# Front of a hybrid encoder layer: values of heads 0-3 ahead of the last convolution chunk, scores that don't wait for values, the squares of the queries by one operation

## The chip, the cores and the metric

The kernel runs on one core of one Trainium2 chip. The metric is the device time of one execution in microseconds (us), lower is better. The kernel before was run three times: 1312.26 us in the median, 1311.49 to 1314.74.

## What is computed

One encoder layer over 256 rows of 2048 numbers, all in float32 (cut to what matters here):

```python
u = rms_norm(h) @ w_in                      # 2048 -> 5120
u_conv, u_attn = split(u)                   # 2 x 1024 | queries, keys, values: 3 x 1024
# group A: a * sigmoid(b), 31 taps along the rows, layer norm, silu
# group B: 8 heads, each with two sets of queries and keys of 64, values of 128
q, k = rms_norm(q) / 8, rms_norm(k)         # over each 64
p = softmax(where(mask, q @ k.T, -inf))     # two maps a head
o = rms_norm((p[0] - lam * p[1]) @ v)       # over each 128
h = h + concat([conv, o]) @ w_out           # 2048 -> 2048
y = h + moe(rms_norm(h))                    # 32 experts, the top 2 of one of 4 groups
```

## The kernel before

The kernel has a front (norm, input projection, convolution, attention, output projection, router) and a back, in which 16 pairs of experts pass one after another: every pair streams its gate, up and down weights through a ring of nine tiles of 2 MB, and its matmuls follow the loads. The ring's tiles are buffers of the front, reused: a load starts when the front has let go of its buffer (lines 979 to 1010).

**Steps.** The front's two projections are 112 steps. Steps 0 to 79 are the input projection: ten groups of 512 columns, eight steps each, in the order that ORDER (line 26) gives. A group is a convolution chunk ("c", 256 of the 1024 channels with their gates), or queries, keys or values of four heads ("q", "k", "v"; 0 is heads 0-3, 1 is heads 4-7). Steps 80 to 111 are the output projection: part 0 (heads 0-3, steps 80 to 87), part 1 (heads 4-7, 88 to 95) and part "c" (the convolution, 96 to 111), each over four groups of 512 columns. Weights come in tiles of 2 MB, one for four steps. A step has 12 matmuls of 512 columns (lines 714 to 716): float32 is split into a rounded half and its rest, and three products of the four are taken. The split of a step's weights (`split`, lines 665 and 666) is a copy on ScalarE and a subtraction on VectorE; it is issued two steps ahead, one step ahead in the output projection, into one of three buffers.

**The planner.** All engines but SP run in the order in which the code issues instructions, and everything besides steps is issued by a small planner while the kernel is built. Work is a set of generators ("units"), each of which yields the engine it needs next (A ScalarE, D VectorE, P TensorE) with a cost in us, and waits by W (a number of steps) or C (a condition of the plan; no engine waits there). In each step `vector_phase` adds PACE_A to ScalarE's room and PACE_V to VectorE's, and what TensorE's own units took before, and issues units in order of priority while there is room; unused room is not kept. VectorE's room that no unit needs goes to taps of the convolution (`fill`, TAP us each; 31 taps for each of 8 blocks of 128 channels, line 325, the first of a block line 322), from one list in the order of the chunks. After a step's matmuls `tensor_phase` issues P units that are ready. A unit that changes its engine goes on one step later at the earliest, except P of a "quick" one.

**Units of the change.** `queries` (lines 433 to 452): for each of two tiles of 128 rows a scaled copy out of PSUM (441), then `squares` (line 430): for each of eight pieces of 64 columns one Square on ScalarE that also sums; the inverse roots for the scale of the scores by bit tricks and three Newton steps on GpSimd (146 to 150, 169 to 171); four transposes (420) and copies (451). `keys` (454 to 478): squares, inverse roots, scaled by VectorE (466), transposed. `values` (480 to 485): a scaled copy. `attend` (one for tile 0, two for tile 1, for each set of four heads): scores by matmul (499), mask and negative maximum on VectorE (506 to 508), exponential with its sum on ScalarE (517), the difference of the two maps on VectorE (525 to 534), transposes (540), a copy (544), the product with the values (554). `attend_norm`: squares of the result (430 again), inverse root on GpSimd, scale (570, 572), transposes (420), rounded half (579) and rest (581) for the output projection. `conv_norm` takes the mean over channels when the last taps are done (362, 366), subtracts it (370), squares, variance (381), inverse root (390), and `conv_out` finishes in four pieces (403 to 410). `finish` adds the projection to the input rows (611), transposes the sum (617) for the router (626).

**What waits.** Before each part of the output projection the plan waits (`idle_until`) until both norms of that part's heads, or a piece of the convolution, have been issued: rounds without a step, each with two warming matmuls (line 245) and room of 2.5 us for ScalarE and VectorE.

Of the kernel before, what the change touches and what calls it, by code (L numbers as in the profile page):

```python
# [14 lines left out]
AF = mybir.ActivationFunctionType  # L15
ALU = mybir.AluOpType
AX = mybir.AxisListType

EPS = 1e-6
S, D = 256, 2048  # L20
NT = 2
# [1 line left out]
DC = 1024  # L23
TAPS = 31

ORDER = [('c', 0), ('c', 1), ('c', 2), ('k', 0), ('k', 1), ('q', 0), ('c', 3), ('v', 0), ('q', 1), ('v', 1)]
NH, HD, VD = 8, 64, 128
NE, NG, EPG = 32, 4, 8
DE = 512
# [1 line left out]
C = 64  # L31
LAM_INIT = 0.8 - 0.6 * math.exp(-0.3 * 0)
NEG = -1.0e30
PACE_A, PACE_V = 1.3, 1.25
PARTS = (0, 1, "c")
TAP = 0.38
IDLE = 2.5
SC_AT = 4
PIECES = ((0, 256), (256, 384), (384, 512))
# [18 lines left out]
def block_kernel(ctx, tc, x, xT, par, w_in, w_out, w_gu, w_dn, out):  # L58
# [81 lines left out]
    def tmp(shape=(128, 512)):  # L140
        i = free_tmps.pop(0)
        return i, wk.tile(list(shape), F32, name=f"t{i}", bufs=1)
# [281 lines left out]
    def squares(ps, ssq, scale):  # L424

        i, sq = tmp()
        w = 512 // ssq.shape[1]
        for j in range(ssq.shape[1]):
            c = slice(j * w, (j + 1) * w)
            nc.scalar.activation(sq[:, c], ps[:, c], AF.Square, scale=scale(j), accum_out=ssq[:, j:j + 1])  # L430
        free_tmps.append(i)

    def queries(half, ps):

        ssq = sm.tile([128, NT * 8], F32, name="qs")
        hs = slice(4 * half, 4 * half + 4)
        ys = []
        for t in range(NT):
            yield "A", 2.9, 2
            i, y = tmp()  # L440
            nc.scalar.activation(y, ps[t][1], AF.Copy, scale=rstd1[:, t:t + 1])
            squares(ps[t][1], ssq[:, 8 * t:8 * t + 8], lambda j: rstd1[:, t:t + 1])
            free_banks.append(ps[t][0])
            if t == 1:
                rstd_bits(ssq, HD, rq[:, half].rearrange("p t h r -> p (t h r)"), "k", nc.gpsimd)
            yield "P", 1, 0.44
            b0, tv = turn(y, i)
            yield "A", 1.1, 0
            for r in range(2):
                p = slice(64 * r, 64 * r + 64)  # L450
                nc.scalar.activation(qz[r][p, hs, t * 128:(t + 1) * 128], tv[p], AF.Copy, scale=qg[p, 0:1])
            free_banks.append(b0)

    def keys(half, ps):
        ssq = sm.tile([128, NT * 8], F32, name="qs")
        hs = slice(4 * half, 4 * half + 4)
        for t in range(NT):
            yield "A", 2.3, 1
            squares(ps[t][1], ssq[:, 8 * t:8 * t + 8], lambda j: rstd1[:, t:t + 1])
        rk = rstd_bits(ssq, HD, sm.tile([128, NT * 8], F32, name="rk"), "k", nc.gpsimd)  # L460
        yield "W", 2
        ys = []
        for t in range(NT):
            yield "D", 0.65, 1
            ys.append(tmp())
            nc.vector.scalar_tensor_tensor(ys[t][1].rearrange("p (h d) -> p h d", d=HD),
                                           ps[t][1].rearrange("p (h d) -> p h d", d=HD), rstd1[:, t:t + 1],
                                           rk[:, 8 * t:8 * t + 8, None].to_broadcast([128, 8, HD]),
                                           op0=ALU.mult, op1=ALU.mult)
            free_banks.append(ps[t][0])  # L470
        tvs = []
        for t in range(NT):
            yield "P", 1, 0.44
            tvs.append(turn(ys[t][1], ys[t][0]))
        for t in range(NT):
            yield "A", 0.6, 0
            nc.scalar.activation(kT[:, hs, t * 128:(t + 1) * 128], tvs[t][1], AF.Copy, scale=P("kg"))
            free_banks.append(tvs[t][0])
# [8 lines left out]
    def attend(t, g, s, st):  # L487

        nk = t + 1
        K = nk * 128  # L490
        nh = 4 // nk
        h0 = 4 * g + s * nh
        yield "P", 2, 0.9
        pv = []
        for r in range(2):
            b0, ps = bank()
            v = ps.rearrange("p (h k) -> p h k", k=K)
            for j in range(nh):
                nc.tensor.matmul(v[:, j], qz[r][:, h0 + j, t * 128:(t + 1) * 128], kT[:, h0 + j, 0:K],  # L499
                                 start=True, stop=True)  # L500
            pv.append((b0, v))
        nm = sm.tile([128, 2, 2, 4], F32, name="nm", bufs=4)
        for r in range(2):
            yield "D", 1.0, 0
            b0, v = pv[r]
            nc.vector.memset(v[0:64, :, K - 64:K], NEG)
            nc.vector.tensor_reduce(nm[:, r, 0, :nh], v, axis=AX.X, op=ALU.max, negate=True)
            nc.vector.tensor_tensor(nm[:, r, 1, :nh], nm[:, r, 0, :nh], rq[:, g, t, s * nh:s * nh + nh, r],
                                    op=ALU.mult)
        pe = []  # L510
        for r in range(2):
            yield "A", 0.25 * nh + 0.6, 2 - r
            b0, v = pv[r]
            i, p = tmp()
            pp = p.rearrange("p (h k) -> p h k", k=K)
            for j in range(nh):
                nc.scalar.activation(pp[:, j], v[:, j], AF.Exp, bias=nm[:, r, 1, j:j + 1],
                                     scale=rq[:, g, t, s * nh + j, r:r + 1],
                                     accum_out=esum[:, t, r, h0 + j:h0 + j + 1])
            free_banks.append(b0)  # L520
            pe.append((i, pp))
        yield "D", 1.4, 0
        (i0, p0), (i1, p1) = pe
        c = sm.tile([128, 2, 4], F32, name="c", bufs=4)
        nc.vector.reciprocal(c[:, 0, :nh], esum[:, t, 1, h0:h0 + nh])
        nc.vector.scalar_tensor_tensor(c[:, 1, :nh], c[:, 0, :nh], nlam, esum[:, t, 0, h0:h0 + nh],
                                       op0=ALU.mult, op1=ALU.mult)
        for j in range(nh):
            nc.vector.scalar_tensor_tensor(p0[:, j], p1[:, j], c[:, 1, j:j + 1], p0[:, j],
                                           op0=ALU.mult, op1=ALU.add)  # L530
        free_tmps.append(i1)
        if s == t:
            st["rs0"] = sm.tile([128, 4], F32, name="rs0", bufs=4)
            nc.vector.reciprocal(st["rs0"], esum[:, t, 0, 4 * g:4 * g + 4])
        yield "P", 1, 0.44
        b0, tp = bank()
        tv = tp.rearrange("p (h k q) -> p h k q", k=nk, q=128)
        for j in range(nh):
            for kt in range(nk):
                nc.tensor.transpose(tv[:, j, kt], p0[:, j, kt * 128:(kt + 1) * 128], ident)  # L540
        free_tmps.append(i0)
        yield "A", 0.6, 1
        i, at = tmp()
        nc.scalar.activation(at, tp, AF.Copy)
        free_banks.append(b0)
        av = at.rearrange("p (h k q) -> p h k q", k=nk, q=128)
        yield "P", int("po" not in st), 0.9
        if "po" not in st:
            st["po"] = bank()
        for j in range(nh):  # L550
            h = h0 + j
            o = st["po"][1][:, (s * nh + j) * 128:(s * nh + j + 1) * 128]
            for kt in range(nk):
                nc.tensor.matmul(o, av[:, j, kt], vt[:, kt, h * VD:(h + 1) * VD],
                                 start=kt == 0, stop=kt == nk - 1)
        free_tmps.append(i)
# [125 lines left out]
    if True:  # L682
        for j, (key, lhs, kb0, k, pk, first, last) in enumerate(steps):
# [37 lines left out]
            if pk[0] == "in":  # L721
                kind, half = ORDER[pk[1]]
                gen = {"c": gated, "q": queries, "k": keys, "v": values}[kind](half, ps[pk])
                acts[kind, half] = start(gen, 1, lambda: "n1" in acts and acts["n1"]["end"] and acts["sc"]["end"])
                if kind == "v":
                    g = half
                    for t in range(NT):
                        st = {}
                        subs = [start(attend(t, g, s, st), 2 + g, lambda g=g: all(
                            acts[x, g]["end"] for x in "qkv") and len(free_tmps) >= 3) for s in range(t + 1)]  # L730
                        acts["n", t, g] = start(attend_norm(t, g, st), 2 + g,
                                                lambda subs=subs: all(u["end"] for u in subs))
            elif pk[1] < 2:
                start(add_part(pk[2], ps[pk]), 1)
            else:
                for t in range(NT):
                    start(finish(pk[2], t, ps[pk][t]), 1, quick=True)
        nc.scalar.activation(dummy, eps_c, AF.Sqrt)
        idle_until(lambda: not units)

# [469 lines left out]
```

## Time and profile before

| | |
|---|---|
| median of three runs | 1312.26 us (1311.49 to 1314.74) |
| profiled execution | 1314.85 us, span of its instructions 1312.9 us |
| TensorE busy | 1236.6 us, 94% of the span |
| VectorE, ScalarE busy | 514.1 us, 296.2 us |
| read from HBM | 466.17 MB, 357 GB/s over the span |
| front, to the first matmul of the first expert's gather | 387.5 us |

The busy shares are means over stages with different limits: before 390 us the three engines are busy together, behind it VectorE and ScalarE have little to do and the DMA is full. In rows of the trace, columns are: start us, duration us, engine, line, operation, output<-inputs, count, and in brackets the idle time before it and what ended it.

### The profile page before, as it was taken

How to read it: one execution, taken by the hardware profiler on the slowest of the kernel's cores; microseconds unless marked ns; L12 is line 12 of the kernel's file. 1: busy time of each engine (PE TensorE's matmuls, PEld its weight loads, DVE VectorE, ACT ScalarE, POOL GpSimd, SP SyncE). 2: the span in 40 equal slices, each digit the busy share in tenths (PEclk: the TensorE clock that was granted, in tenths of full speed). 3: DMA queues.
4: the chain of work that ended last, by engine and by line, in shares of the span. 5: the costliest groups of instructions: out<-in, count | busy, mean ns of one | idle time of the engine just before them, and what ended most of it. 6: DMA issues, size and time to landing. Idle time of an engine off the chain costs nothing.

```text
span 1312.9 us, 15143 instructions
## 1 busy us (share of the span) xinstructions
PE 1236.6 (94%) x6299; PEld 702.0 (53%) x6299; DVE 514.1 (39%) x992; ACT 296.2 (23%) x574; POOL 48.0 (4%) x116
## 2 busy tenths in 40 slices
PE   7999999899999999999999898989989898989997
PEld 5887788787884453553525344342525344342533
DVE  6898898997551130321303123030303022130313
ACT  6446647565430010110101001010101001010101
POOL 2001210420000000000000000000000000000000
PEclk9999999999999999999999999999999999999999
DMA  9444553745658999999999999999999999999996
GB/s 384 185 182 167 190 192 136 291 188 193 254 222 359 427 427 428 428 426 430 427 427 429 427 428 426 428 427 428 427 427 429 426 428 428 426 429 426 428 427 242
DMA packets 37033, 469.30 MB, mean 357 GB/s; under 512 B 4192, under 2 KB 4960, under 8 KB 8160
## 3 DMA queue, kind: packets, MB, share of 16 engines
q1 hardware_dynamic: 35808, 466.63, 85.4%
q10 hardware_dynamic: 1152, 1.65, 0.4%
q8 instruction: 51, 0.84, 0.3%
q14 instruction: 22, 0.18, 0.0%
HBM read 466.17 MB, written 2.10 MB: 357 GB/s over the span
## 4 chain that ended last, share of the span: by engine, by line
PE 61%; DMA 33%; DVE 2%; ACT 1%; POOL 1%; issue 0%; ACTq 0%; SPq 0%; DVEq 0%
DMA v<-in_w_gu_dram 28%; PE b L882 13%; PE b L920 13%; PE b L863 8%; PE b L716 6%; PE b L714 6%; PE b L715 6%; PE b L947 4%; DMA v<-in_w_dn_dram 3%; DMA v<-in_w_in_dram 1%; PE b L499 1%; ACT u L665 1%; DMA v<-in_xT_dram 1%; ACT t L430 1%; DVE u L666 1%; PE b L626 1%
## 5 line engine op out<-in xcount | busy, mean ns | idle before, releaser
L882 PE MATMUL b<-v,u 128*64 128x512 f32 x2048 | 452.4, 594 | 45.5 <-DMA v<-in_w_gu_dram 45.4
L882 PEld LDWEIGHTS b<-v,u 128*64 128x64 f32 x2048 | 142.9, 137 | 349.6 <-issue 264.2
L891 DVE TENSOR_TENSOR hid<-sil,b 64x512 f32<-64x512 f32 x32 | 21.9, 685 | 517.5 <-ACT sil L890 517.4
L920 PE MATMUL b<-v,hT 128*64 128x512 f32 x992 | 217.2, 594 | 1.7 <-DMA v<-in_w_dn_dram 1.3
L714 PE MATMUL b<-u,v 128*128 128x512 f32 x448 | 180.0, 402 | 9.3 <-ACT u L665 8.6
L716 PE MATMUL b<-u,v 128*128 128x512 f32 x448 | 176.9, 395 | 1.8 <-DVE v L581 1.8
L715 PE MATMUL b<-u,v 128*128 128x512 f32 x448 | 176.4, 394 | 0.8 <-DVE u L666 0.8
L666 DVE TENSOR_TENSOR u<-v,u 128x1024 fp32r<-128x1024 f32 x112 | 136.9, 1224 | 55.4 <-ACT u L665 54.6
L665 ACT ACTIVATE u<-v 128x1024 fp32r<-128x1024 f32 x112 | 119.0, 1065 | 141.5 <-PE b L716 107.1
L920 PEld LDWEIGHTS b<-v,hT 128*64 128x64 f32 x992 | 69.8, 137 | 134.5 <-issue 133.6
L890 ACT ACTIVATE sil<-b,sv 64x512 f32<-64x512 f32 x32 | 21.8, 682 | 527.7 <-PE b L882 503.2
L863 PEld LDWEIGHTS b<-dg,xs 128*128 128x128 f32 x1024 | 121.1, 192 | 14.8 <-issue 11.9
L863 PE MATMUL b<-dg,xs 128*128 128x128 f32 x1024 | 125.5, 276 | 0.6 <-DVE dg L843 0.4
L928 ACT ACTIVATE u<-b,sv 128x512 fp32r<-128x512 f32 (+1 forms) x66 | 44.4, 674 | 245.0 <-PE b L920 193.7
L714 PEld LDWEIGHTS b<-u,v 128*128 128x128 f32 x448 | 85.6, 191 | 26.3 <-ACT u L665 8.6
L325 DVE SCALAR_TENSOR_TENSOR v<-v,pr 128x255 f32<-128x255 f32 (+14 forms) x240 | 97.1, 465 | 0.0
L716 PEld LDWEIGHTS b<-u,v 128*128 128x128 f32 x448 | 85.2, 190 | 20.9 <-DVE v L581 2.9
L715 PEld LDWEIGHTS b<-u,v 128*128 128x128 f32 x448 | 85.5, 191 | 19.0 <-DVE u L666 2.1
L929 DVE SCALAR_TENSOR_TENSOR u<-b,sv,u 128x512 fp32r<-128x512 f32 (+1 forms) x66 | 48.2, 732 | 109.5 <-ACT u L928 109.5
L947 PE MATMUL b<-u,dwT 128*128 128x512 f32 (+2 forms) x264 | 76.7, 412 | 0.2 <-DVE u L948 0.2
L865 DVE TENSOR_TENSOR u<-b,g2v 128x512 f32<-128x512 f32 x64 | 44.3, 692 | 29.8 <-PE b L863 29.4
L948 DVE TENSOR_TENSOR u<-u,b 128x512 f32<-128x512 f32 (+2 forms) x62 | 41.2, 664 | 30.1 <-PE b L947 30.1
(200 smaller groups left out, 565.6 us busy)
## 6 DMA issues: line engine op xcount, KB each, us to landing
v<-in_w_gu_dram SPq DMA_DIRECT2D x125, 2048.0 KB, 32.5
v<-in_w_dn_dram SPq DMA_DIRECT2D x60, 2048.0 KB, 35.4
v<-in_w_in_dram SPq DMA_DIRECT2D x18, 2048.0 KB, 7.9
v<-in_w_out_dram SPq DMA_DIRECT2D x8, 2048.0 KB, 8.1
v<-in_w_gu_dram SPq DMA_DIRECT2D x6, 1024.0 KB, 12.5
v<-in_w_dn_dram SPq DMA_DIRECT2D x5, 1024.0 KB, 9.1
v<-in_w_in_dram SPq DMA_DIRECT2D x8, 512.0 KB, 9.3
v<-in_xT_dram SPq DMA_DIRECT2D x4, 512.0 KB, 8.7
```

What stands on the lines that cost most here:

```text
L325: nc.vector.scalar_tensor_tensor(cacc[:, b, d:], hb[:, b, :S - d], ck[:, b, j:j + 1], cacc[:, b, d:], op0=ALU.mult, op1=ALU.add)
L665: nc.scalar.activation(sp[:, 0], w, AF.Copy)
L666: nc.vector.tensor_tensor(sp[:, 1], w, sp[:, 0].bitcast(F32), op=ALU.subtract)
L714: nc.tensor.matmul(o, lh, sp[:, 0, k2], start=first and k2 == 0, stop=False)
L715: nc.tensor.matmul(o, lh, sp[:, 1, k2], start=False, stop=False)
L716: nc.tensor.matmul(o, ll, sp[:, 0, k2], start=False, stop=last and k2 == 1)
L863: nc.tensor.matmul(tv[:, k], xs[:, t, (k0 + k) * 128:(k0 + k + 1) * 128], dg[:, t].rearrange("p i c -> p (i c)"), start=t == 0, stop=t == 1)
L882: nc.tensor.matmul(gu[i][h:h + 64], tT[:, kb, i * C:(i + 1) * C], w[:, k2, g], start=kb == 0, stop=kb == KB - 1, skip_group_check=True)
L920: nc.tensor.matmul(ps[64 * i:64 * i + 64], hT[:, f, i], columns(wd[i], f), start=f == 0, stop=f == 3, skip_group_check=True)
L928: nc.scalar.activation(y[:, 0, a:b], ps[:, :b - a], AF.Copy, scale=sv[:, 0:1])
L929: nc.vector.scalar_tensor_tensor(y[:, 1, a:b], ps[:, :b - a], sv[:, 0:1], y[:, 0, a:b].bitcast(F32), op0=ALU.mult, op1=ALU.subtract)
L947: nc.tensor.matmul(ps[:, :b - a], dwT[:, t], y[:, k, a:b], start=k == 0, stop=k == 1)
```

## The change

The group of values of heads 0-3 changes places with convolution chunk 3 in ORDER, and the columns of the input weights with it (`layout` follows ORDER). The queries' squares become one Square of the whole tile into a scratch tile and one sum over eight pieces on VectorE, and their PSUM bank is given back before it. Attention units are started when the queries' group has been projected, tile 1 first, and begin when queries and keys of their heads are done; a condition ahead of the product waits for the values. `attend_norm` is started with the values as before. Keys yield one step ahead of their transposes. `finish` is quick for the last two column groups only. PACE_V goes from 1.25 to 1.4, TAP from 0.38 to 0.40.

```diff
-ORDER = [('c', 0), ('c', 1), ('c', 2), ('k', 0), ('k', 1), ('q', 0), ('c', 3), ('v', 0), ('q', 1), ('v', 1)]
+ORDER = [('c', 0), ('c', 1), ('c', 2), ('k', 0), ('k', 1), ('q', 0), ('v', 0), ('c', 3), ('q', 1), ('v', 1)]
...
-PACE_A, PACE_V = 1.3, 1.25
+PACE_A, PACE_V = 1.3, 1.4
...
-TAP = 0.38
+TAP = 0.40
...
-            yield "A", 2.9, 2
+            yield "A", 1.3, 2
             i, y = tmp()
             nc.scalar.activation(y, ps[t][1], AF.Copy, scale=rstd1[:, t:t + 1])
-            squares(ps[t][1], ssq[:, 8 * t:8 * t + 8], lambda j: rstd1[:, t:t + 1])
             free_banks.append(ps[t][0])
+            i2, sq = tmp()
+            nc.scalar.activation(sq, y, AF.Square)
+            nc.vector.tensor_reduce(ssq[:, 8 * t:8 * t + 8], sq.rearrange("p (j d) -> p j d", j=8),
+                                    axis=AX.X, op=ALU.add)
+            room["D"] -= 0.7
+            free_tmps.append(i2)
...
         tvs = []
+        yield "W", 1
         for t in range(NT):
             yield "P", 1, 0.44
             tvs.append(turn(ys[t][1], ys[t][0]))
...
+        yield "C", lambda: ("v", g) in acts and acts["v", g]["end"]
         yield "P", int("po" not in st), 0.9
...
+                if kind == "q":
+
+                    st, g = [{} for _ in range(NT)], half
+                    subs = [[start(attend(t, g, s, st[t]), 2 + g, lambda g=g: all(
+                        acts[x, g]["end"] for x in "qk") and len(free_tmps) >= 3) for s in range(t + 1)]
+                            for t in reversed(range(NT))][::-1]
                 if kind == "v":
-                    g = half
                     for t in range(NT):
-                        st = {}
-                        subs = [start(attend(t, g, s, st), 2 + g, lambda g=g: all(
-                            acts[x, g]["end"] for x in "qkv") and len(free_tmps) >= 3) for s in range(t + 1)]
-                        acts["n", t, g] = start(attend_norm(t, g, st), 2 + g,
-                                                lambda subs=subs: all(u["end"] for u in subs))
+                        acts["n", t, g] = start(attend_norm(t, g, st[t]), 2 + g,
+                                                lambda subs=subs[t]: all(u["end"] for u in subs))
...
-                    start(finish(pk[2], t, ps[pk][t]), 1, quick=True)
+                    start(finish(pk[2], t, ps[pk][t]), 1, quick=pk[2] >= 2)
```

## Rows read from the trace of the kernel before

**Rows 1.** Chain of waits, whole span, in order of time: start, us, what.

```profile
446.61 27.47 PE b L882 x128
...
500.03 27.47 PE b L882 x128
...
713.78 32.47 DMA v<-in_w_gu_dram
```

**Rows 2.** Busy time by stretch: stretch, length, engines, granted clock, DMA share, GB/s.

```profile
390.00:400.00 10.00, 10.00 (x68) 6.46 (x68) 4.64 (x20) 0.41 (x2) 0.00 (x0) 1.00 0.22 70
```

**Rows 3.** Same view, columns PE, PEld, DVE, ACT, POOL, clock, DMA, GB/s.

```profile
40.00:248.00 208.00, 205.89 (x958) 170.71 (x957) 182.12 (x342) 121.40 (x280) 30.47 (x69) 1.00 0.46 171
...
294.00:306.00 12.00, 9.90 (x45) 7.87 (x45) 9.95 (x16) 4.73 (x8) 0.00 (x0) 0.86 0.29 123
```

**Rows 4.** Chain of waits, 240 to 310 us: between the two projections.

```profile
248.51 2.59 PE b L362 x12
251.10 5.24 PE b L499 x32
...
256.84 0.67 PE b L420 x4
...
265.50 0.67 DVE v L581
...
268.92 0.23 PE b L716
```

**Rows 5.** The same chain, ahead of part 1 of the output projection.

```profile
293.66 0.89 PE b L245 x8
294.55 3.47 PE b L381 x16
...
302.15 0.67 DVE v L581
...
306.21 0.23 PE b L714
```

**Rows 6.** TensorE's waits, 40 to 390 us: total us, times, longest.

```profile
PE b L420 <- DVE t L466: 2.0, 2, 1.1
...
PE b L617 <- DVE xs L611: 1.1, 3, 0.4
```

**Rows 7.** Timeline of GpSimd: first and last of 13 operations of one norm.

```profile
288.55 0.19 POOL L169 TENSOR_SCALAR ov<-os 128x4 f32<-128x4 f32 x1 [4.02 <-ACT t L430]
...
293.22 0.20 POOL L150 TENSOR_TENSOR oy<-oh,oy 128x4 f32<-128x4 f32 x1
```

**Rows 8.** Taps (line 325) by stretch: VectorE busy (count), clock, DMA, GB/s.

```profile
248.00:294.00 46.00, 13.64 (x35) 0.93 0.64 249
```

**Rows 9.** Timelines of ScalarE and VectorE: chunk 3 is ready; its first taps.

```profile
180.54 0.58 ACT L349 ACTIVATE v<-b 128x512 f32<-128x512 f32 x1
...
224.26 0.73 DVE L322 TENSOR_SCALAR v<-v,pr 128x256 f32<-128x256 f32 x2
```

**Rows 10.** Timeline of VectorE: the last tap, the first finished pieces of the convolution.

```profile
288.24 0.45 DVE L325 SCALAR_TENSOR_TENSOR v<-v,pr 128x226 f32<-128x226 f32 x1
...
312.72 1.29 DVE L410 TENSOR_TENSOR v<-v,v 128x512 fp32r<-128x512 f32 x2
```

**Rows 11.** Groups of instructions, 0 to 640 us: busy us, mean ns, idle before.

```profile
L430 ACT ACTIVATE t<-b,rstd 128x64 f32<-128x64 f32 x64 | 19.1, 339 | 0.0
...
L507 DVE TENSOR_REDUCE nm<-b 128x2 f32<-128x512 f32 (+1 forms) x12 | 8.3, 692 | 0.4
...
L602 ACT ACTIVATE t<-xs 128x512 f32<-128x512 f32 x4 | 2.5, 620 | 4.7 <-DVE xs L611 4.7
```

**Rows 12.** Timeline of ScalarE around the first exponential.

```profile
202.60 1.06 ACT L665 ACTIVATE u<-v 128x1024 fp32r<-128x1024 f32 x1 [5.19 <-PE b L716]
203.68 1.28 ACT L517 ACT_TABLE_LOAD   x1
204.98 0.46 ACT L517 ACTIVATE t<-b,nm,rqs 128x128 f32<-128x128 f32 x1
```

## The prediction

> **What bounds the kernel now.** I read four views in this order. First the chain of waits in order of time, over the whole span. From 394.88 us on it is one pattern repeated for 16 pairs of experts: until about 656 us matmuls of the gate and up product, 53.4 us from pair to pair, and from then on 31 to 41 us of waiting for expert weights in each (one such row stands for all) [rows 1]. TensorE waits at the end of every pair, so this stage is bound by its weights. What starts that stream? At 390 to 400 us the DMA stands almost still, at 70 GB/s: all buffers of the ring are full, and the next load waits until the first expert has used one [rows 2]. So whatever ends the front (everything before 387 us) earlier or later moves the end by the same amount, one for one.
>
> Second, busy time by stage. In the projection, 40 to 248 us, TensorE is busy 205.89 of 208 us, VectorE 182.12 [rows 3]. The front is TensorE's; it can only get shorter by its gaps, its warming matmuls and its half clock. Third, the chain inside the front shows where these are. **Wait 1**: the input projection ends at 248.06, the first step of the output projection at 269.15. Of these 21.1 us, 2.6 (means of the convolution), 5.2 (scores of heads 4-7), 0.7 (turning an output) and one step of 2.7 (12 matmuls of 0.23) are work; **9.9 us are lost**, and the chain leaves it through the last VectorE instruction of heads 0-3's output, L581 [rows 4]. **Wait 2**: from 293.66, the end of step 87, to 306.2, the end of step 88, are 12.5 us, of which 3.5 (variances), 0.4 (turning) and 2.7 (the step) are work; **5.9 us are lost**, again up to an L581, this time of heads 4-7 [rows 5]. Fourth, TensorE's list of waits: 2.0 us for the scaled keys, twice, and 1.1 us for the sum before a transpose, three times [rows 6]. Everything that this change can win is 9.9 + 5.9 + 2.0 + 1.1 = 18.9 us.
>
> **The change part by part.**
> *Keys.* The new W lets the transposes of the keys be issued one step later, behind work that is ready. 2.0 us go [rows 6]. What is late next: keys by 2.7 us, which nobody uses before the scores, more than a group later.
>
> *Values of heads 0-3 one group earlier, attention without waiting for them.* In planner steps before: the queries of heads 0-3 are complete at step 52, but scores wait until the values at step 64 (196 us). After: the scores start at 52, and with the same 16 steps of stages (scores, maximum, exponential, difference, transpose, copy, product, norm) heads 0-3 end near step 68, 12 before the output projection needs them. Wait 1 goes whole: **-9.9**. The 5.2 us of scores of heads 4-7 move into the projection and still cost 5.2; they are not a gain. The new condition "values ready" holds up nothing: it is the planner's, no engine waits in it, and values are copied (1.3 us) 4 steps after the queries end, two before the product is due. The DMA order of the projection's weights stays, only their columns are exchanged; the loads into attention's buffers, in SP's queue, are released earlier, never later.
>
> *Heads 4-7.* Their queries end at step 76 (one earlier than now, as the squares cost the planner 1.3 rather than 2.9). Their scores then start at 76, where now they start in the first idle round. 16 steps later is 92, but the output projection wants them at step 88. So **a wait 2 remains, and now more of the late work falls into it**. What has to pass there? Chain alone: the last norm is issued in step 87, so its squares run 1.7 us ahead of the end; the inverse root on GpSimd takes 4.9 us [rows 7], the rest (scale, transpose, copy, residue) some 3.5 with hand-overs: 8 us after step 87. By VectorE's queue: taps of the convolution left then, the last two additions of part 0 (1.3), two norms (3.2), the subtraction of the mean (2.5).
>
> *How many taps are left?* Before, 35 taps run after 248 us, at 0.39 us each [rows 8]. After: pace 1.4 for 1.25 gives 0.15 x 70 steps = +10.5 units of VectorE to the planner by then; the price 0.40 for 0.38 on 206 taps takes 4.1, the queries' reductions 2.8, heads 4-7's maxima and first difference 7.4, the rest of heads 0-3 2.1, and TensorE's longer phases give back some 2.5. Net -3.4 units, 8 or 9 taps: about 43 left at step 80. Eight steps take 26 of them, beside the other units; 16 or 17 remain, 6.4 us. VectorE's sum in wait 2 is 6.4 + 1.3 + 3.2 + 2.5 = 13.4, say 14 us with hand-overs. Bounds for wait 2 are thus 8 and 14; I take 12, nearer the upper one, since VectorE was busy in 9.95 of 12 us in the same place before [rows 3]. Of the 12, 1.3 are work (a transpose and the last mean), and the half clock after it costs 1.2, as in step 88 now: 11.9 lost for 5.9: **+6.0**.
>
> *Is chunk 3 of the convolution too late?* It moves back by one group of 8 steps. Its input lies ready at 180.5 us now, but VectorE, still behind, touches it first at 224.3 [rows 9]. 44 us of slack cover a shift of 22. At nothing; without that cover each step it is late costs 1.4 units of taps. From the last tap (288.2) to the first finished piece (313.3) are 25 us [rows 10]; with taps ending near 291 to 293, pieces come at 316 to 318, and TensorE reaches that part at 281 + 12 + 1.2 + 8 x 2.72 + 3.5 = 319.5. Just in time.
>
> *Squares by one operation.* 4 tiles x 8 x (a square and its read-out, 0.29 apart) = 9.3 us leave ScalarE, 4 x 0.62 return; 4 reductions of 0.69 come to VectorE [rows 11]. ScalarE's part lies beside matmuls; VectorE's 2.8 us are in the count of taps. The reduction's price is that of 512 elements in the row, 0.692.
>
> *Tables.* The sigmoid of chunk 3 now lies between two sets of exponentials: two more table loads, 1.28 us each. The row shows the load beginning 0.02 us after the copy before it and the exponential 0.02 us after its end [rows 12]: 0 (covered) to 2.6 us; I take 0, as ScalarE waits for matmuls most of the time, and keep 2.6 in the range. The Trainium skill (ScalarE: Activation LUTs, What ACT_TABLE_LOAD costs) tells to group calls by set, and gives 2.66 us a switch with a drain of 1.38 in it: by it the two cost at most 5.3 and the sum below would be -1.3. This trace agrees with the load (1.28) and shows no drain beside it.
>
> *The end.* Additions of parts n < 2 no longer share a step with their transposes: two of three waits of 0.4 go, **-0.7** [rows 6].
>
> Sum: -2.0 - 9.9 + 6.0 - 0.7 = **-6.6 us**. The profiled execution took 1314.85 (span 1312.9 and 1.95 around it), which gives 1308.2; it lies 2.6 above the median of 1312.26, against which the forecast is **1305.7 us**.
>
> **The rivals.** (A measurement of this kernel tells some 0.3%, 3.9 us, from no change.)
> *Both waits go.* If attention of heads 4-7 closes in 12 steps rather than 16, nothing is left to wait for: -2.0 - 9.9 - 5.9 - 0.7 = -18.5, 1294; halfway, 1298. For it: ScalarE is freed of 7 us. Against it: VectorE has no room.
> *The convolution becomes the bound.* If the last tap falls after 295 us (10 taps more than counted), part three waits for its pieces; at 300 it starts at 325, as now, and only the 0.7 at the end remains: 1311. For it: my count of taps is a difference of large numbers, and VectorE is asked for more. Against it: the slack of 44 us.
> *Slower: VectorE overfilled in the projection.* A step has 2.72 us. A split takes 1.23, and 1.4 units of taps 1.38: 2.61. But a unit of 1.0 of attention takes 1.3 in truth, so a step full of those needs 3.05, 0.33 too much. Splits are two steps ahead, so it decides once the lag passes 2.7 us; if all 32 steps of attention paid it, 10.6 us, and with wait 2 at 14 the sum is +6: 1318. Against it: 26 us of VectorE are free between 40 and 248 [rows 3], and steps with scores are longer than 2.72.
> That the change doesn't do what it says I rule out: scores of heads 0-3 can't wait for values in the new order.
>
> **How the numbers follow.** Forecast 0.50, with wait 2 from 8 to 14 and tables 0 to 2.6: 1301.5 to 1310. Both waits shrink 0.18 (1294 to 1301). Convolution bound 0.18 (1309 to 1313). VectorE overfilled 0.14 (1314 to 1320). The range reaches from 1298 to 1313, leaving out under half of the second and the last. Below 1308.3: 0.44 of the first and all of the second, 0.62. Within 0.3%: 0.06, the third and 0.01 of the last, 0.25. Slower: 0.13.
>
> **What would show it.** Right: no warming matmuls between the projections, the first output step right behind step 79, near 252 us; a gap up to an L581 after step 87 of 8 to 14 us; taps ending inside that gap; after 40 us three table loads for sigmoid and exponential where one was; the first gate and up matmul near 388 us. Wrong: gaps of TensorE behind L666 between 140 and 250 us, a gap before the convolution's part, or a front that moves without the end moving by the same.

## The result, and the profile after

The changed kernel takes **1305.24 us** (median of 5 runs, 1304.69 to 1305.62), the kernel before 1311.94 in its 5 runs: ratio 0.9948 (95% interval 0.9936 to 0.996), a gain of 0.5%. The profiled execution has a span of 1303.3 us. The kernel before was run and profiled once more beside the experiments (e5, median 1312.05 us); that execution's span is 1309.8, where the one shown ahead of the prediction had 1312.9. **Of the 3.1 us that the first profile was slower, 2.5 lie in the first steps behind its two waits**: step 80 took 5.8 us in it and 4.7 in the second, step 88 took 7.1 and 5.7. Within these steps TensorE waits equally long in both; what differs is its clock. The first profile runs most of step 80 and the second half of step 88 at half clock (0.50 granted); the second profile is back at full clock halfway through step 80 and runs all of step 88 at full clock. One row of each covers step 88: [rows 3] has a mean clock of 0.86 from 294 to 306 us, and the second profile of before has 1.00:

```profile
294.00:306.00 12.00, 9.91 (x49) 7.89 (x49) 10.07 (x15) 5.92 (x10) 0.00 (x0) 1.00 0.18 75
```

So the second profile, which lies at the median, is the one to compare with. Line numbers are those of the kernel named beside them; after has other numbers than before.

Where the two traces part, and where they run together again, by the starts of TensorE's steps (us):

| | before, second profile | after | difference so far |
|---|---|---|---|
| step 46 (keys done) | 143.12 | 141.41 | -1.7 |
| end of step 79 (input projection) | 248.11 | 252.12 | +4.0 |
| step 80 (output projection, part 0) | 263.44 | 251.95 | -11.5 |
| end of step 87 | 292.66 | 279.73 | -12.9 |
| step 89 | 303.58 | 298.63 | -5.0 |
| step 96 (convolution's part) | 322.62 | 317.67 | -5.0 |
| end of step 111 | 376.66 | 370.08 | -6.6 |
| first gate and up matmul | 392.24 | 385.66 | -6.6 |

From the first gate and up matmul to the end of the span it is 917.6 us in both, so all that the change gains lies in the front, and it passes to the end one for one. The chain of waits of each kernel shows that matmul. Second profile of before:

```profile
392.24 27.62 PE b L882 x128
```

After:

```profile
385.66 27.62 PE b L891 x128
```

Busy time by stretch, after (length, PE, PEld, DVE, ACT, POOL, clock, DMA share, GB/s), against [rows 3]:

```profile
40.00:252.00 212.00, 211.57 (x997) 176.48 (x996) 191.49 (x366) 121.15 (x236) 32.98 (x78) 1.00 0.47 171
252.00:280.00 28.00, 28.00 (x141) 23.64 (x140) 26.65 (x58) 16.48 (x41) 3.56 (x13) 1.00 0.83 342
280.00:296.00 16.00, 10.50 (x59) 9.52 (x58) 13.40 (x30) 7.49 (x17) 4.62 (x13) 0.79 0.44 165
```

TensorE is busy in 239.57 of the 240 us from 40 to 280; what it loses stands in 280 to 296, where the clock falls to 0.79 on average. There VectorE is the full engine: 13.40 of 16. TensorE's waits between 40 and 390 us, the whole list, against [rows 6]:

```profile
PE b L366 <- DVE v L325: 5.5, 1, 5.5
PE b L793 <- DVE A L789: 0.6, 1, 0.6
PE b L420 <- DVE t L471: 0.4, 1, 0.4
PE b L872 <- DVE dg L852: 0.2, 1, 0.2
```

Keys wait 0.4 us where they waited 2.0, the three waits before transposes at the end are gone, and one new wait stands at the head: the convolution's second mean (366) for the last taps (325). Chain of waits of after through wait 2, against [rows 5]:

```profile
279.73 0.90 PE b L561 x8
...
280.66 1.51 ACT t L430 x8
...
282.25 1.52 POOL ov L169
...
287.12 0.74 DVE v L325 x2
...
287.90 2.07 PE b L366 x4
289.97 0.85 PE b L245 x4
290.82 0.85 PE b L420 x4
...
292.57 3.46 PE b L381 x16
296.03 0.23 PE b L721
```

After the last product of attention (561) the chain goes through the norm's squares (ScalarE) and its inverse root (GpSimd) to VectorE's taps, then to the mean, which comes at half clock like the turning behind it (0.85 us for four instead of 0.44), and to the variances (381).

### The profile page after: what moved, and what is told of

Read it like the earlier page. It is cut to its first block, busy times and chain, and to the rows that moved or that the text cites. A ratio compares the mean times of both kernels' runs of the same rounds, so it can differ in the third digit from the quotient of the medians.

```text
span 1303.3 us, 15071 instructions
## 1 busy us (share of the span) xinstructions
PE 1231.6 (94%) x6291; PEld 700.8 (54%) x6291; DVE 515.6 (40%) x996; ACT 291.7 (22%) x516; POOL 46.8 (4%) x116
## 4 chain that ended last, share of the span: by engine, by line
PE 65%; DMA 31%; DVE 2%; ACT 1%; POOL 1%; issue 0%; SPq 0%
DMA v<-in_w_gu_dram 28%; PE b L891 13%; PE b L929 13%; PE b L872 8%; PE b L722 7%; PE b L723 7%; PE b L721 7%; PE b L956 4%; DMA v<-in_w_dn_dram 3%; PE b L505 1%; PE b L633 1%; PE b L907 0%; ACT t L430 0%; DMA v<-in_w_in_dram 0%; PE b L561 0%; DVE u L673 0%
## 5 line engine op out<-in xcount | busy, mean ns | idle before, releaser
L874 DVE TENSOR_TENSOR u<-b,g2v 128x512 f32<-128x512 f32 x64 | 44.3, 692 | 29.7 <-PE b L872 29.2
```

## The experiments

Twelve kernels ran; the changed kernel (after) is the base of each but e5, which is the kernel before once more (its profile is the second one above). Ratios are to the kernel before, with 95% intervals.

| | edit | us | ratio |
|---|---|---|---|
| e1 | old order | 1311.05 | 0.9989 (0.998 to 0.9998) |
| e2 | scores wait for values | 1322.11 | 1.0078 (1.0064 to 1.0092) |
| e3 | old pace and price of taps | 1321.07 | 1.0069 (1.0054 to 1.0084) |
| e4 | old squares | 1316.07 | 1.0033 (1.0022 to 1.0043) |
| e5 | kernel before again | 1312.05 | 0.9998 (0.9989 to 1.0007) |
| e6 | keys' W and `quick` undone | 1307.15 | 0.9961 (0.9948 to 0.9975) |
| e7 | 16 taps less | 1314.39 | 1.0016 (1.0007 to 1.0025) |
| e8 | pace 1.6 | 1314.47 | 1.0017 (1.0008 to 1.0026) |
| e9 | pace 1.6, mean later | 1309.15 | 0.9979 (0.997 to 0.9988) |
| e10 | 16 taps less, mean later | 1307.51 | 0.9972 (0.9961 to 0.9983) |
| e11 | old squares, mean later | 1305.88 | 0.9946 (0.9932 to 0.9959) |
| e12 | e9 with norms first | 1300.11 | 0.9911 (0.9897 to 0.9924) |

**e1: the order back, early scores kept.**

```
-ORDER = [..., ('q', 0), ('v', 0), ('c', 3), ('q', 1), ('v', 1)]
+ORDER = [..., ('q', 0), ('c', 3), ('v', 0), ('q', 1), ('v', 1)]
```

> The changed kernel with the groups in the old order (convolution chunk 3 ahead of the values of heads 0-3); scores still start without values. Theory (early scores make the gain, the order adds nothing): scores of heads 0-3 start at step 52 as in the changed kernel, products at 64 to 66 when the values are there, norms near step 73, still before step 80: wait 1 stays gone, wait 2 stays 16 us, 1305 +- 1.5 us. Rival (the order makes the gain): heads 0-3 come late again and wait 1 is back, 1310 to 1314 us.

It lost 5.8 of the 6.7 us, but at none of the places named. Wait 1 stays away (step 80 starts 0.2 us ahead of the modelled end of step 79), and the gap between steps 87 and 88 is 16.6 us against 15.9. The loss is inside the projection: steps 68 to 71 end at 229.34 us, in after at 223.99. The products of heads 0-3 now wait for their values and are issued together at step 64, so both norms follow each other directly on GpSimd, at 205.6 and 211.6 us; in after they start there at 190.5 and 204.8. VectorE's timeline there (e1):

```profile
207.79 0.17 DVE L170 TENSOR_SCALAR oi<-ov 128x4 int32<-128x4 int32 x1
...
211.86 0.17 DVE L170 TENSOR_SCALAR oi<-ov 128x4 int32<-128x4 int32 x1 [3.70 <-POOL ov L169]
...
212.15 1.23 DVE L673 TENSOR_TENSOR u<-v,u 128x1024 fp32r<-128x1024 f32 x1
```

The second norm's shift (170) stands first in VectorE's queue and waits 3.70 us for GpSimd, which is still at the Newton steps of the first norm. The split of the next weights (673) stands behind it, and TensorE has nothing to multiply. TensorE's waits (e1) show two that are not in after, beside the same 5.5 us at the mean:

```profile
PE b L420 <- DVE t L579: 2.2, 2, 1.6
PE b L722 <- DVE u L673: 1.0, 1, 1.0
```

These waits (3.2 us) and the lower clock after them (0.84 granted from 220 to 230 us, 1.00 in after) make the 5.3 us; the longer gap behind step 87 adds 0.7. So the new order pays its 5.8 us by keeping two norms apart, not by bringing heads 0-3 in earlier. That is read from this trace; no run has the old order with the norms held apart.

**e2: scores wait for their values again, new order.**

```
-                        acts[x, g]["end"] for x in "qk") and len(free_tmps) >= 3) for s in range(t + 1)]
+                        (x, g) in acts and acts[x, g]["end"] for x in "qkv") and len(free_tmps) >= 3) for s in range(t + 1)]
```

> The changed kernel with the old condition: scores start only when the values of their heads are there; the new order is kept. Theory: heads 0-3 start at step 56 and are in time, no wait 1; heads 4-7 start at step 80 instead of 76, so their norms end four rounds later and wait 2 grows from 16 to 20 to 24 us, while 5.2 us of scores leave the projection for the output steps: 1309 to 1313 us. Rival (the order makes the gain): 1305 us.

The direction holds, the size does not: scores of heads 4-7 come at steps 80, 82 and 86, the gap between steps 87 and 88 is 33.6 us. TensorE's waits name the norm (420 <- 579) 8.3 us. The kernel is 16.9 us slower than after, more than twice the whole change. Not all of that need be the price of late scores: the convolution's mean starts here at step 78 (245.34 us), ahead of them, and by e4 to e11 below that delays scores by itself. How the 16.9 us divide between the two was not tried.

**e3: the old pace** (`PACE_V` 1.25, `TAP` 0.38).

> The changed kernel with PACE_V 1.25 and TAP 0.38. Theory: some 16 more taps (6.4 us) are left at step 88 and lengthen wait 2 by 4 to 6 us: 1309 to 1311 us. Rival (the higher pace overfills VectorE and costs in the projection): faster than the changed kernel, 1300 to 1304 us.

It came out 10 us above the theory's range. Taps (line 325) of e3 by stretch (DVE busy, clock, DMA share, GB/s):

```profile
40.00:252.00 212.00, 77.71 (x191) 1.00 0.46 169
252.00:280.00 28.00, 3.86 (x10) 1.00 0.90 357
280.00:310.00 30.00, 15.18 (x40) 0.77 0.32 115
```

50 taps are left at 252 us, 40 of them after 280. The gap behind step 87 is 19.6 us, the variances come only behind step 90 (3.1 us between steps), and 5.4 us are lost ahead of step 96, the first of the convolution's part. Here the prediction's second rival is real: the convolution is the bound. And the keys wait again, though their W is still there:

```profile
PE b L420 <- DVE t L471: 2.0, 2, 1.1
```

**e6: the two small parts undone** (without the W in `keys`; `quick=True` for all parts).

> The changed kernel without the keys' step of waiting and with all additions quick. Theory: 2.0 us of waits at the keys and 0.7 to 1.6 in the last part come back: 1307.5 to 1309 us. Rival (those waits were covered by wait 2 anyway, which VectorE ends): 1305 to 1306 us.

The time is 1.9 us up, 1307.15 us, but only one of the two parts brings it. TensorE's waits (e6):

```profile
PE b L623 <- DVE xs L617: 1.0, 3, 0.4
...
PE b L420 <- DVE t L471: 0.4, 1, 0.4
```

**The keys' waits do not come back.** Without the W their transposes stay in steps 37 and 45, as in after, and step 46 starts 29.7 us behind step 36 in both. The plan says why: a unit that changes its engine goes on one step later at the earliest, so a W of 1 between VectorE's scaling and the transposes adds nothing. What moved the transposes is the pace with its price of taps. At 1.4 and 0.40 the second scaling falls into the step after the first, and the transposes come behind both; at 1.25 and 0.38 (before without the W, e3 with it) and at 1.6 and 0.40 (e8 and e9, with it) both scalings fall into one step, the transposes are issued in steps 36 and 44, and 1.9 to 2.0 us of waits stand there. The whole loss of e6 lies behind step 96 (2.2 us from there to the end of step 111): it is the price of quick additions.

**e4, e7, e8: three ways to change VectorE's load.** e4 puts the old squares back (the sum leaves VectorE, the planner's price is 2.9 again), e7 leaves 16 taps away, e8 raises the pace (cut to the lines that say it):

```
-            yield "A", 1.3, 2
+            yield "A", 2.9, 2
...
+            squares(ps[t][1], ssq[:, 8 * t:8 * t + 8], lambda j: rstd1[:, t:t + 1])
...
```
```
-    conv_left = [8 * TAPS]
+    conv_left = [8 * TAPS - 16]
...
-        for j in range(TAPS - 1, -1, -1):
+        for j in range(TAPS - 1, 7 if n == 3 else -1, -1):
```
```
-PACE_A, PACE_V = 1.3, 1.4
+PACE_A, PACE_V = 1.3, 1.6
```

> The changed kernel with the old squares of the queries (eight Squares with sums on ScalarE, cost 2.9). Theory: heads 4-7 start one step later (+1 to +2.7 us), VectorE is relieved of 2.8 us (-2.8 us in wait 2): 1303 to 1307 us, no difference that can be told. Rival (the squares on ScalarE were what held up the queries): 1309 us or more.

> The changed kernel with 16 taps of the convolution's chunk 3 left out (8 of 31 for each of its two blocks; the output is another). Theory (VectorE's queue and the chain of heads 4-7's norm both end near the same time in wait 2): the last tap comes 6 us earlier, wait 2 falls from 16 to 11 to 13 us, held by the norm's chain: 1300.5 to 1303 us. Rival A (VectorE's queue alone): 1299 us. Rival B (the norm's chain alone): 1305 us.

> The changed kernel with PACE_V 1.6. Theory (VectorE is 90% busy in the projection, so little more fits; taps come at most 20 us of busy time earlier): wait 2 shrinks by 2 to 4 us, gaps of TensorE behind the splits stay under 1.5 us: 1301 to 1304 us. Rival (VectorE overfilled): splits come late, gaps of TensorE behind the subtraction of the split of 4 us and more in the projection, 1306 to 1312 us.

All three missed on the wrong side: **with less work on VectorE, or the same work earlier, the kernel was 9 to 11 us slower**. Gap between steps 87 and 88: 22.2, 26.4 and 22.5 us for 15.9. TensorE's timeline of e8 shows the scores (505) of heads 4-7 and the convolution's first mean (362):

```profile
235.16 2.75 PE L362 MATMUL b<-v,mean_w 128*128 128x256 f32 x12
...
243.70 1.89 PE L505 MATMUL b<-v,v 128*128 128x256 f32 x8
...
250.88 1.89 PE L505 MATMUL b<-v,v 128*128 128x256 f32 x8
...
261.25 1.95 PE L505 MATMUL b<-v,v 128*128 128x128 f32 x16
```

After, for comparison:

```profile
238.53 3.61 PE L505 MATMUL b<-v,v 128*128 128x256 f32 x16
...
247.43 1.95 PE L505 MATMUL b<-v,v 128*128 128x128 f32 x16
...
261.05 2.76 PE L362 MATMUL b<-v,mean_w 128*128 128x256 f32 x12
```

In after, two units of scores go at step 76 and the rest at 78; the mean comes behind them, at 82. In e8, and likewise in e7 and e4, one unit goes at 76, the next at 78 and tile 0 only at step 81, 14 us late. The mean starts when fewer than 31 taps are left (line 686), and it holds its PSUM bank until the last tap is in (355 to 371). A unit of scores takes two banks, and during steps the planner keeps two free (236). Whoever finishes taps sooner starts the mean sooner, and its bank is missing to the scores. That was the new theory; the rival was that VectorE's queue, not the bank, holds the scores. Counted through the plan of the code, all three units of scores are ready at step 76 in after and in e8; six banks are free then in after, which lets two units go, and five in e8, which lets one go.

**e9, e10, e11: the same three with the mean later.** One line in each:

```
-    acts["cn"] = start(conv_norm(), 0, lambda: conv_left[0] < 31)
+    acts["cn"] = start(conv_norm(), 0, lambda: conv_left[0] < 8)
```

> As e8 (PACE_V 1.6), but the convolution's mean starts, and takes its PSUM bank, at 8 taps left instead of 31. Theory (in e8 the mean's bank, taken at step 74, kept the scores of tile 0 of heads 4-7 from starting until step 81): two attention units start at 76, the third at 78, as in the changed kernel, and wait 2 falls from 22.5 to 11 to 14 us; the 2 us at the keys stay lost: 1303 to 1306 us. Rival (VectorE overfilled, or the convolution's normalisation with its higher priority goes ahead of the norms): wait 2 stays 20 us or more, 1312 us or more.

> As e7 (16 taps of chunk 3 left out), with the mean at 8 taps left. Theory: scores again at 76 and 78, the last tap 6 us earlier than in the changed kernel, wait 2 of 11 to 13 us, held by the chain of the norm: 1300.5 to 1303.5 us. Rival (the convolution's normalisation ahead of the norms): wait 2 of 20 us or more, 1308 us or more.

> As e4 (old squares on ScalarE), with the mean at 8 taps left. Theory (e4 lost through the bank, since 2.8 us less of reductions let VectorE reach the last 31 taps before step 76): scores of tile 0 at 78 or 79 instead of 81, wait 2 from 22.2 to 13 to 16 us, 1303 to 1307 us. Rival (the squares themselves hold up the queries): 1312 us or more.

The scores are back at steps 76 and 78 in all three, with pace, taps and squares left as they were, and the line alone is worth 5.3 us (e8 to e9), 6.9 (e7 to e10) and 10.2 (e4 to e11). TensorE's timeline of e9:

```profile
240.41 3.61 PE L505 MATMUL b<-v,v 128*128 128x256 f32 x16
...
249.31 1.95 PE L505 MATMUL b<-v,v 128*128 128x128 f32 x16
...
270.21 2.75 PE L362 MATMUL b<-v,mean_w 128*128 128x256 f32 x12
```

So the bank is shown. e11 differs from after by the old squares and the later mean together, and is 0.6 us slower, with runs from 1302.5 to 1307.69: no worth of the squares by one operation can be told here. e11 fell into its range; e9 and e10 missed theirs by 3 and 4 us, and one more wait says why. e9's list of waits begins with it:

```profile
PE b L723 <- DVE v L588: 4.9, 1, 4.9
PE b L420 <- DVE t L579: 2.1, 2, 1.4
PE b L420 <- DVE t L471: 2.0, 2, 1.0
```

Step 88 has begun (at 293.0 us) and its third matmul waits 4.9 us for the residue of heads 4-7 (588); the next five come at half clock (0.43 us each for 0.23). In e9's chain of waits it stands behind the convolution's reciprocal (390, 146) and scaling (403), which have priority 0 where the norms have 3:

```profile
291.84 1.67 DVE t L390
...
295.54 2.40 DVE v L403 x4
297.94 0.67 DVE v L588
...
298.66 0.79 PE b L723
```

**e12: norms of heads 4-7 first.** e9, with

```
-    acts["cn"] = start(conv_norm(), 0, lambda: conv_left[0] < 8)
+    acts["cn"] = start(conv_norm(), 4, lambda: conv_left[0] < 8)
...
+        yield "C", lambda: all(("n", t, 1) in acts and acts["n", t, 1]["end"] for t in range(NT))
         yield "A", 1.0, 3
...
-            acts["cy", g] = start(conv_out(g, cr), 0)
+            acts["cy", g] = start(conv_out(g, cr), 4)
...
-        yield "W", 1
+        yield "W", 2
```

> As e9 (PACE_V 1.6, the convolution's mean at 8 taps left), and: the convolution's normalisation has a lower priority than attention and goes on to its square root only when the norms of heads 4-7 have been issued; keys wait two steps ahead of their transposes instead of one. Theory (in e9 and e10 step 88 waited 4 to 5 us for the last residue of heads 4-7, which stood behind the convolution's reciprocal and scaling in VectorE's queue): that wait goes, wait 2 lasts 9 to 11 us up to a step 88 of normal length, the 2 us at the keys go, and no step waits for the convolution's pieces: 1301 to 1304 us. Rival (pieces come too late instead): a gap ahead of step 96 of 3 us or more, 1305 us or more.

It took 1300.11 us, a little under the theory's range, and is faster than after by 5.1 us and than the kernel before in the runs beside it (1311.67) by 11.6. The gap between steps 87 and 88 is 6.8 us, step 88 takes 3.4. Busy time by stretch (e12), beside the rows of after above:

```profile
40.00:252.00 212.00, 211.97 (x997) 176.62 (x996) 196.07 (x381) 121.06 (x235) 32.46 (x78) 1.00 0.47 171
252.00:282.00 30.00, 29.66 (x149) 24.81 (x148) 29.02 (x64) 18.76 (x50) 5.13 (x14) 1.00 0.89 350
282.00:296.00 14.00, 13.89 (x74) 11.62 (x74) 7.76 (x13) 8.69 (x14) 2.87 (x13) 1.00 0.33 132
```

VectorE does 15 operations more before 252 us, and in 282 to 296 TensorE is busy in 13.89 of 14 us at the full clock. From what is left of the list of waits (e12):

```profile
PE b L723 <- DVE u L674: 1.5, 2, 1.1
...
PE b L366 <- DVE v L325: 0.3, 1, 0.3
```

The mean's wait of 5.5 us in after is 0.3 (e9 had it at 0.4 already), and the keys' waits are gone: a W of 2 does move the transposes one step later. From the first gate and up matmul to the end of the span it is again 917.7 us, so all of it was gained in the front. Which of e12's own parts (priorities, condition, W) brings how much was not tried apart.

## Why the prediction was right

The forecast was 1305.7 us and the time is 1305.24; the sum was -6.6 us, and against the second profile of before the first gate and up matmul comes 6.6 us sooner. Wait 2 stands on the mechanism named, wait 1 on half of it and the keys' term on none of it, and that the total comes so close is luck in part. Term by term, with the second profile of before as the base:

| term | predicted | measured |
|---|---|---|
| keys | -2.0 | -1.7 |
| wait 1 | -9.9 | -8.8 |
| wait 2 | 11.9 for 5.9: +6.0 | 10.1 for 4.3: +5.8 |
| end | -0.7 | -1.6 |
| rest, spread over steps 46 to 87 | 0 | -0.3 |

*The base.* Wait 1 lost 9.9 us in the first profile and 8.8 in the second (248.11 to the end of step 80 at 268.1, less the same 11.2 of work); wait 2 lost 5.9 and 4.3 (292.66 to 303.58, less 6.6 of work). In after it lost 10.1: 279.73 to 298.63, less 8.8 of work, as a product, a second turning and the last mean now fall into it too. The prediction took the 2.6 us by which its profile lay above the median off at the end, as if they lay where the change doesn't reach. Most of them lay in the waits that it changes, so against that profile the change is worth 9.6 us of span (1312.9 to 1303.3), not 6.6. That the total is right to half a microsecond is luck: three sizes were off in directions that cancel, wait 1 by 1.1 too much, both ends of wait 2 by 1.6 and 1.8 too much, the end by 0.9 too little.

*Keys.* The number is near, **the mechanism is wrong**. The prediction gave the 2.0 us to the new W; e6 shows that the W does nothing at this pace, and e3 that the waits return with the old pace and price although the W is there. The -1.7 belongs to the pace with its price of taps, which the prediction counted only as taps.

*Wait 1 goes.* Right, and from the step named: scores of heads 0-3 at steps 52 and 54, their last residue in step 70 (predicted: near 68), step 80 right behind step 79. **Wrong is what the prediction put it on.** It moved the values ahead of chunk 3 so that heads 0-3 are ready; e1 shows that early scores do that alone, and that the order pays elsewhere, by 5.8 us, and by e1's trace through two norms that no longer meet on GpSimd. The sum had no term for it since it was made for both edits at once: a right sum with a wrong share.

*Wait 2 remains, and VectorE decides.* Right: VectorE is the engine that is full, and the last tap ends at 288.2 us, behind two additions and a residue of heads 4-7 that stand between the taps, as counted. But attention's own chain was no 8 us either: GpSimd's inverse root ended at 288.26 us, level with the taps, and the last residue (588) at 294.5, 14.8 us after step 87. The sign that the prediction set, a gap of 8 to 14 us up to that residue, was missed: the gap between the steps is 15.9 us, no matmul waits for the residue in after's list, and the convolution's variances, which end later still, at 296.03, set step 88. The stretch without the variances took 12.5 us for the 12 taken (295.68 - 279.73 - 3.46). What was off lies around it: a product and a second turning (0.89 + 0.44) pass in it too, which are work, and step 88 came at full clock (2.95 us for 2.72), as half clock was spent ahead of it, on the mean, the warming and the turning (0.50 granted from 287.9 to 291 us, 1.00 from 292 on). Taps, after, by stretch:

```profile
40.00:252.00 212.00, 83.70 (x206) 1.00 0.47 171
252.00:280.00 28.00, 7.37 (x19) 1.00 0.83 342
280.00:310.00 30.00, 6.06 (x16) 0.89 0.43 158
```

35 were left at step 80 (predicted 43), 19 were taken in its eight steps (predicted 26), 16 remained, as predicted: two misses that cancel. Pace and price gained 15 taps up to 252 us (50 left in e3, 35 here), and the prediction had given them 16 (10.5 - 4.1 units of 0.40); so what it counted against them, 25 taps, was 15. That the eight steps had less room because half of heads 4-7's chain falls into them is read from the timeline and wasn't tried.

*Chunk 3 isn't late, at nothing.* Right: there is no wait for the convolution ahead of step 96 in after's list. It was close, as predicted: the last finished piece (line 410) ends at 316.3 us, step 96 starts at 317.67. The rival shows itself once 50 taps are left (e3).

*Tables at nothing.* Right. Three loads where one was (ScalarE's timeline, after), and TensorE's list has no wait for ScalarE:

```profile
168.98 1.28 ACT L523 ACT_TABLE_LOAD   x1
...
201.22 1.28 ACT L334 ACT_TABLE_LOAD   x1
...
245.99 1.28 ACT L523 ACT_TABLE_LOAD   x1
```

The Trainium skill (ScalarE: Activation LUTs, What ACT_TABLE_LOAD costs) gives 2.66 us a switch with a drain in it, which would make an estimate of 5.3 us for the two; in these rows the next operation begins 0.01 to 0.02 us behind the load, no drain shows, and no wait of TensorE leads to them.

*The end.* This term was mis-sized. All three waits of 0.4 before transposes went, not two, and more than the waits went with them: the three gaps of TensorE around these transposes fell from 1.30, 1.36 and 1.36 us to 0.63 each, 2.1 in all (e6, where the additions are quick again, has the old gaps and loses 2.2). Step 96, which took 0.5 us longer than in before, takes the rest back.

*Squares and pace.* The prediction saw them as taps gained or lost at 0.39 us each. e4, e7 and e8 show that this is not what they do here: in after the mean starts just behind the scores, on the good side of an edge, and 0.2 of pace, 16 taps or the queries' sums carry it over, at 9 to 11 us. The sum had no term for the bank; that after stays on the good side was not foreseen. The rival that feared VectorE overfilled shows in no run: at pace 1.6 the keys' waits are 2.0 us again (e9) and step 46 starts at 143.42 us for 141.41, but by the plan both scalings share a step there, as at pace 1.25, and no split comes late in the projection.

## What to carry to other kernels

A condition that starts an accumulation early also takes its bank early: when a faster engine makes a kernel slower, look at which instructions moved forward, and what they hold that others wait for. Two chains through a slow helper engine can cost little one after the other and much side by side: in e1 VectorE, which takes its work in order, stood 3.70 us behind one result of GpSimd, with the split that TensorE needed next behind it. Undo the small parts of a change one at a time and look where the time comes back: e6 gave back the expected time, but not at the keys. And measure the profile that you make a sum against twice: what a wait loses differed by 1.1 and 1.6 us between two executions of the same kernel.

## What was not expected of the hardware

- GpSimd's small operations (128x4) mostly take 0.20 us but at times 1.0 to 2.1, and these are not random: all six of over 1 us in after end 0.04 to 0.07 us behind the end of an operation of VectorE that ran beside them, a weight split (673) or a run of taps (325). The one at 282.25 us (1.52) ends with the taps that end at 283.71; the one at 205.63 in e1 (2.14) with taps that end at 207.70. In e1 the next stands under the split of 212.15 to 213.38 us:

```profile
212.33 1.10 POOL L146 TENSOR_TENSOR oh<-oy 128x4 f32<-128x4 f32 x1 [0.50 <-DVE oy L171]
```

  The 13 operations of one norm took 6.0 us in after (282.25 to 288.26) and 4.9 before [rows 7]. The profile's spans on GpSimd are rough.
- How long half clock lasts after a wait varies for the same work: behind the same waits, step 80 of the kernel before took 5.8 us in one profile and 4.7 in the other, step 88 7.1 us with half clock (0.50) in its second half and 5.7 at full clock, 2.1 of waits in it; a step without waits takes 2.72 at full clock.
- A load of ScalarE's table costs 1.28 us and nothing measurable beside it: the next operation begins 0.01 to 0.02 us behind it, in after (170.27 behind 168.98 + 1.28, for one) and in before [rows 12].
